# Block sums of the merge formed during the attention, another sequence of the seven products, output sums on VectorE

## The chip, the cores and the metric

One NeuronCore of one Trainium2 chip runs the whole kernel. The metric is the device time of one execution in microseconds (us). TensorE does the matrix products; VectorE (DVE in the rows), ScalarE (ACT) and GpSimd (POOL) work beside it, and SyncE (SP) issues nearly all transfers.

## What is computed

One layer of a hybrid mixer over 1024 tokens of width 1024, in float32. Four branches (A sparse, B sliding window, C stick-breaking, D retention) are gated, projected, merged and projected once more:

```python
h = rms_norm(x, norm_g) * (1.0 + scale) + shift
...
for i, (y, z) in enumerate(branches):
    yi = y.reshape(B, S, BRANCH_W) * jax.nn.silu(z)
    term = jax.nn.sigmoid(h @ w_merge[i]) * (yi @ w_br[i])
    merged = term if merged is None else merged + term
return x + gate * (merged @ w_out)      # and a last rms_norm with final_g
```

The four products `h @ w_merge[i]` and the last one with `w_out`, each 1024 x 1024 x 1024, are what the change is about.

## The kernel before

**Precision.** Every float32 factor is held as a sum of two parts, a rounded one (`hi`) and the rest (`lo`), and a product is three matmuls: hi·hi, hi·lo, lo·hi. To split a block of 128 x 512, ScalarE copies it into `hi` and VectorE or GpSimd subtracts to get `lo` (`parts`, line 1582; `op`, line 1623).

**Three stages.** First the attention stage: projections of `h` (called items), the attention units of the branches, and the z items, which multiply a branch by its gate and store A, B and D to DRAM (`yd`, line 666). Then the merge stage. Then the output stage with `w_out`.

**Seven products for eight.** In merge and output the 2 x 2 block product is done with seven block products instead of eight. The moving side (blocks b11, b12, b21, b22 of `h`, in `hh` and `hl`, line 1566) needs four sums of blocks: T1 = b12 - b11, T2 = b22 - T1, T3 = b22 - b12 and T4 = b21 - T2. `t_jobs` (line 1592) forms the first three when the merge stage begins, four slices of 512 columns each, in SBUF tiles `tt`; `t4_jobs` (line 1654) puts T4 in the place of b12 during the first pair. Because b12 is needed whole again at the end, its sum hi + lo is stored in DRAM (`hd`) and split again later (line 1841).

**The order of the merge.** The merge has 32 tiles of 128 output rows (4 branches x 8). Four of them (`PLAIN`, line 38) are done as ordinary products: two at the start (line 1720), two at the end (line 1826), 2 x (24 + 6) matmuls of 512 columns each. The other 28 are 14 pairs (line 1735); a pair is seven products of 12 matmuls (`product`, line 1679) and four terms of 6 (`br_term`, line 880). The sums of products of a pair are formed as they come out of PSUM: five additions on VectorE, two on GpSimd, and two copies on ScalarE.

**Output stage.** The four blocks of `w_out` are loaded into `wr` (line 1801) once the T tiles are free, that is after the fifth of the last pair's seven products (T3's). `w_jobs` (line 1800) forms their sums while the last two plain tiles run; some go where parts of `h` were, so they wait for the tile that read those. The output is then four pairs of seven products (line 1901). `gated` (line 1878) multiplies by the gate on VectorE and adds x, on GpSimd in three pairs of four; `norm` (line 1886) uses GpSimd for two multiplications and ScalarE for the scaling.

**What sets the order.** In each stage the program notes its instructions and `Program.schedule` (line 293) lists them by a cost model: at each step the engine that is free earliest takes its ready instruction of smallest rank. A rank is the place in the program plus a shift by label, from two long tables (`SHIFT_PE`, `SHIFT`, lines 99 to 151). What is issued is one fixed order for each engine, DMA issues on SP and GpSimd included. An instruction that waits holds up all that stands behind it on its engine.

Of the kernel before, what the change touches and what calls it, by code (L numbers as in the profile page):

```python
# [88 lines left out]
def chunks(w):  # L89
# [22 lines left out]
    ('first', 0): 300, ('first', 1): 0, ('first', 2): 300, ('first', 4): 9970, ('first', 5): 21923,  # L112
# [3 lines left out]
    ('h1', 7): 0, ('item', 0): 0, ('item', 10): 0, ('item', 11): 43, ('item', 12): 0,  # L116
    ('item', 13): 100, ('item', 14): -100, ('item', 16): -9900, ('item', 17): 10870,
    ('item', 19): 9990, ('item', 2): -10000, ('item', 21): 0, ('item', 22): 0, ('item', 26): 633,
    ('item', 28): 10000, ('item', 30): 9997, ('item', 4): -300, ('item', 5): 9997,
    ('item', 6): 9960, ('item', 7): 9967, ('item', 9): 2077, ('mod', 0): 0, ('mod', 1): 3000,  # L120
    ('mod', 2): 11000, ('mod', 3): 2900, ('mod', 4): -11000, ('mod', 5): -3, ('mod', 6): 0,
    ('mod', 7): 7000,
}
SHIFT = {
# [12 lines left out]
    ('D1', 5): 10173, ('D1', 6): 2990, ('ada', 3): -300, ('ada', 4): 10000, ('ada', 7): -30,  # L137
# [3 lines left out]
    ('item', 1): 10300, ('item', 10): -9910, ('item', 12): 20, ('item', 13): -10320,  # L141
    ('item', 14): -300, ('item', 15): -10997, ('item', 16): 9997, ('item', 18): 0,
    ('item', 19): 1100, ('item', 2): 0, ('item', 20): 0, ('item', 21): 0, ('item', 22): 273,
    ('item', 23): 0, ('item', 24): 100, ('item', 25): -10000, ('item', 26): 19676, ('item', 27): 0,
    ('item', 28): -9700, ('item', 29): -10000, ('item', 3): -3000, ('item', 30): 997,
    ('item', 4): 130, ('item', 5): 0, ('item', 6): 0, ('item', 7): 0, ('item', 8): -10643,
    ('item', 9): -10000, ('mod', 1): -11000, ('mod', 3): 0, ('mod', 4): 1000, ('mod', 5): -10800,
    ('mod', 6): -10980, ('mod', 7): -10000, ('split', 0): 0, ('split', 1): -10000,
    ('split', 2): -3000, ('split', 3): -10000, ('split', 4): -200, ('split', 6): 10300,
    ('split', 7): 21169, ('x', 4): 19990, ('x', 5): 10300, ('x', 6): 0, ('x', 7): -10000,  # L150
# [250 lines left out]
def hybrid_kernel(ctx: ExitStack, tc: tile.TileContext, x, c, w_ada, b_ada, norm_g, w_in, cmp_pos,  # L401
# [140 lines left out]
    hd = dram.tile([P, 4, 512], F32, name="hd")  # L542
# [288 lines left out]
    it_zcd = [z_item(c0 + P * p, br, p) for p in range(2) for br, c0 in (("C", C_Z), ("D", D_Z))]  # L831
# [43 lines left out]
    it_zb[1].after = "B1"  # L875

# [61 lines left out]
    with ac:  # L938
# [588 lines left out]
    with ExitStack() as mc:  # L1527
# [38 lines left out]
        hblk = [[[v[:, 4 * k:4 * k + 4, 512 * n:512 * n + 512] for v in (hh, hl)] for n in range(2)] for k in range(2)]  # L1566
        (b11, b12), (b21, b22) = hblk
# [4 lines left out]
        tstack = ctx.enter_context(ExitStack())  # L1572
        tt = tstack.enter_context(tc.tile_pool(name="tt", bufs=1, side="right")).tile([P, 3, 2, 4, 512], F32R, name="tt")
        T1, T2, T3 = [[tt[:, i, v] for v in range(2)] for i in range(3)]
# [11 lines left out]
        def minus(x, y, k, d, e):  # L1586

            ve.tensor_tensor(d, f(x[0][:, k]), f(y[0][:, k]), ALU.subtract)
            po.tensor_tensor(e, f(x[1][:, k]), f(y[1][:, k]), ALU.subtract)
            ve.tensor_tensor(d, d, e, ALU.add)  # L1590

        def t_jobs():

            for k in range(4):
                t1 = tmp(f"t1_{k}")
                minus(b12, b11, k, t1, tmp(f"t1e_{k}"))
                parts(T1, k, t1, ve)
                yield
                t2 = tmp(f"t2_{k}")
                ve.tensor_tensor(t2, f(b22[0][:, k]), t1, ALU.subtract)  # L1600
                ve.tensor_tensor(t2, t2, f(b22[1][:, k]), ALU.add)
                parts(T2, k, t2, ve)
                yield
            for k in range(4):
                t = tmp(f"b12_{k}")
                po.tensor_tensor(t, f(b12[0][:, k]), f(b12[1][:, k]), ALU.add)
                sy.dma_start(hd[:, k], t)
                t3 = tmp(f"t3_{k}")
                minus(b22, b12, k, t3, tmp(f"t3e_{k}"))
                parts(T3, k, t3, ve)  # L1610
                yield
# [11 lines left out]
        def op(n):  # L1623

            lo, hi = slice(0, 512), slice(512, 1024)
            if n < NP or n >= NP + 4:
                q, x = divmod(n if n < NP else n - NP - 4, 7)
                if n < NP:
                    (a11, a12), (a21, a22) = [[st.q[base + 2 * q + e].t[:, c] for c in (lo, hi)] for e in range(2)]
# [88 lines left out]
        with md.noted(tc, 8000.0):  # L1718
            tj = t_jobs()
            for n, _ in enumerate(run_items(it_m[:2])):  # L1720
                md.step += 1
                if n % 2 == 1:
                    next(tj, None)
# [276 lines left out]
```

## Time and profile before

| what | us |
|---|---|
| median of 3 runs (1114.05 to 1115.0) | 1114.21 |
| the profiled execution | 1112.57 |
| its span, first to last instruction | 1110.8 |

All rows below come from the one profiled execution, with times from its span's start. Its attention stage ends at about 584 us, the merge at about 1004 us. In the rows a name such as `mt<-hh` is output<-input tile, without buffer numbers: `hh`/`hl` hold the two parts of h, `tt` the T tiles, `mt` scratch, `wst` staged weights, `whi`/`wlo` their parts, `wr` the blocks of `w_out`, `w`/`wt` parts of its sums, `acc` the merged result, `z` rows of the output, `yd` the branches in DRAM. L346 and L369 are the lines that issue noted instructions; they are the same for all. A row of waits or idle time names what ended it.

### The profile page before, as it was taken

The page shows a single profiled execution, that of the slowest core. Times are in us where ns is not written, and L with a number is a line of the kernel's source. Part 1 is how long each engine was busy: PE and PEld are TensorE (multiplying, and loading weights), DVE is VectorE, ACT ScalarE, POOL GpSimd, SP SyncE. Part 2 cuts the span into 40 slices and gives each one's busy share as a digit, 9 for nine tenths or more (in the row PEclk, how much of TensorE's full clock was granted, in tenths as well). Part 3 has the DMA queues.
Part 4 walks back from the last instruction along what each step waited for, and adds up shares of the span by engine and source line. Part 5 has one row for each costly group of instructions (what it writes and reads, how often), then busy time and mean ns, then how long its engine had stood idle before and what let it go on. Part 6 is the DMA issues. An engine that isn't in the chain of part 4 may idle for free.

```text
span 1110.8 us, 16056 instructions
## 1 busy us (share of the span) xinstructions
PE 1043.6 (94%) x5391; PEld 877.6 (79%) x5391; DVE 840.1 (76%) x1753; ACT 589.7 (53%) x1293; POOL 600.2 (54%) x591
## 2 busy tenths in 40 slices
PE   5799999999999999999999699999999999995985
PEld 3578887889888888888888478888888888884874
DVE  6868995987467777878849986677785565668998
ACT  4378974995357667768753343333343333344443
POOL 4584214303444556536555653466666566667785
PEclk9799999999999999999999899999999999997998
DMA  9834311103331010113031023322232233331231
GB/s 299 243 114 119 67 39 39 35 8 75 52 86 48 10 49 30 31 33 81 20 98 60 34 62 105 107 69 67 86 91 54 51 90 86 103 134 59 93 115 76
DMA packets 120230, 86.59 MB, mean 78 GB/s; under 512 B 14556, under 2 KB 107796, under 8 KB 120148
## 3 DMA queue, kind: packets, MB, share of 16 engines
q1 hardware_dynamic: 118672, 81.07, 25.7%
q0 software_dynamic: 1408, 4.48, 1.3%
q8 instruction: 42, 0.69, 0.3%
q14 instruction: 40, 0.33, 0.1%
q10 hardware_dynamic: 68, 0.02, 0.0%
HBM read 72.45 MB, written 8.39 MB: 73 GB/s over the span
## 4 chain that ended last, share of the span: by engine, by line
PE 57%; DVE 10%; issue 3%; ACT 2%; POOL 1%; POOLq 0%; ACTq 0%; DVEq 0%
PE d L346 21%; PE s L346 18%; PE t L346 12%; PE y L346 7%; DVE mt L346 4%; DVE acc L346 1%; DVE wlo L346 1%; DVE hl L346 1%; DVE hl L369 1%; DVE tt L346 0%; DVE SP L346 0%; POOL wlo L346 0%; DVE z L346 0%; POOL mt L346 0%; ACT whi L346 0%
## 5 line engine op out<-in xcount | busy, mean ns | idle before, releaser
L346 POOL TENSOR_TENSOR wlo<-wst,whi 128x512 fp32r<-128x512 f32 (+1 forms) x108 | 141.1, 1317 | 154.6 <-ACT whi L346 140.2
L346 PE MATMUL d<-hh,whi 128*128 128x512 f32 x440 | 182.4, 414 | 16.2 <-ACT whi L346 12.6
L346 PE MATMUL d<-hh,wlo 128*128 128x512 f32 x440 | 174.5, 397 | 1.2 <-POOL wlo L346 1.2
L346 PE MATMUL d<-hl,whi 128*128 128x512 f32 x440 | 173.9, 396 | 0.2 <-POOL hl L346 0.2
L346 ACT ACTIVATE whi<-wst 128x512 fp32r<-128x512 f32 (+2 forms) x121 | 89.0, 737 | 117.7 <-DMA wst<-in_w_merge_dram 35.2
L346 PEld LDWEIGHTS d<-hh,whi 128*128 128x128 f32 x440 | 84.0, 191 | 29.6 <-ACT whi L346 13.5
L346 PEld LDWEIGHTS d<-hh,wlo 128*128 128x128 f32 x440 | 83.4, 190 | 20.9 <-POOL wlo L346 1.6
L346 POOL TENSOR_SCALAR SP<-SP,den,gates 128x640 f32<-128x640 f32 (+7 forms) x64 | 49.8, 787 | 86.7 <-DVE den L346 49.5
L346 PEld LDWEIGHTS d<-hl,whi 128*128 128x128 f32 x440 | 84.2, 191 | 12.0 <-POOL hl L346 0.7
L346 DVE TENSOR_TENSOR lo<-t,hi 128x512 fp32r<-128x512 f32 (+2 forms) x132 | 80.5, 624 | 15.7 <-ACT hi L346 14.8
L346 ACT ACTIVATE hi<-t 128x512 fp32r<-128x512 f32 (+3 forms) x148 | 75.2, 526 | 32.2 <-PE t L346 23.5
L346 PE MATMUL s<-hh,whi 128*128 128x512 f32 x200 | 79.3, 396 | 1.0 <-ACT whi L346 1.0
L346 PE MATMUL s<-hh,wlo 128*128 128x512 f32 x200 | 78.5, 393 | 1.8 <-DVE wlo L346 1.8
L346 POOL TENSOR_TENSOR acc<-acc,mt 128x512 f32<-128x512 f32 x44 | 68.1, 1547 | 19.8 <-DVE mt L346 18.9
L346 PE MATMUL s<-hl,whi 128*128 128x512 f32 x200 | 78.1, 392 | 0.0
L346 ACT ACTIVATE SP<-SP,mx 128x257 f32<-128x257 f32 (+9 forms) x96 | 62.3, 651 | 28.7 <-DVE mx L346 22.9
L346 PE MATMUL t<-kbt,SP 128*128 128x128 f32 (+1 forms) x470 | 69.4, 273 | 8.6 <-DMA kbt<-in_kb_dram 6.9
L346 ACT ACTIVATE mt<-mt 128x512 f32<-128x512 f32 x56 | 35.1, 628 | 65.8 <-POOL mt L346 48.4
L346 PEld LDWEIGHTS t<-kbt,SP 128*128 128x128 f32 (+1 forms) x470 | 55.5, 141 | 16.0 <-DMA kbt<-in_kb_dram 6.9
L346 PE MATMUL s<-tt,whi 128*128 128x512 f32 x176 | 55.7, 398 | 2.9 <-ACT whi L346 2.9
L346 POOL TENSOR_TENSOR mt<-mt,mt 128x512 f32<-128x512 f32 x34 | 49.9, 1467 | 9.0 <-DVE mt L346 7.8
L346 ACT ACTIVATE t<-t 128x512 f32<-128x512 f32 (+5 forms) x97 | 50.2, 524 | 1.3
(365 smaller groups left out, 2946.2 us busy)
## 6 DMA issues: line engine op xcount, KB each, us to landing
wst<-in_w_merge_dram SPq DMA_DIRECT2D x32, 512.0 KB, 4.3
wst<-in_w_in_dram SPq DMA_DIRECT2D x26, 512.0 KB, 3.8
FA<-in_w_ada_dram SPq DMA_DIRECT2D x10, 512.0 KB, 6.0
FA<-in_x_dram SPq DMA_DIRECT2D x8, 512.0 KB, 4.7
pst<-in_w_br_dram SPq DMA_DIRECT2D x32, 128.0 KB, 2.2
ga<-in_w_ada_dram SPq DMA_DIRECT2D x16, 256.0 KB, 3.0
wr<-in_w_out_dram SPq DMA_DIRECT2D x4, 1024.0 KB, 9.1
z<-in_x_dram SPq DMA_DIRECT2D x8, 512.0 KB, 3.8
```

The source lines that it names most:

```text
L346: fn(*args, **kw)
L369: return f(*a, **k)
```

## The change

1. **Block sums in the attention stage.** `t_unit` forms all four sums, slice by slice, after the second z item, splits them and stores both parts in DRAM (`td`, 32 stores of 256 KB). Its scratch is the room of branch D's results, so the z items of D now come ahead of those of C. b12's two parts are stored as they are (`hd`, 2 stores of 1 MB). At the start of the merge six loads of 1 MB bring T2, T1 and T3 into SBUF; two bring T4 over b12 after the two plain tiles; two bring b12 back near the end, without a new split. `t_jobs` and `t4_jobs` are gone.
2. **Another sequence of the products.** T3's product comes third and T1's fifth (`TURN`). All seven sums are VectorE additions with an input in PSUM; the two GpSimd additions and one of the ScalarE copies are gone.
3. **w_out.** T1 has a room of its own; the room of T2 and T3 is given up after the last pair's third product, and the four loads of `w_out` are noted there, ahead of its other four products. w11's parts go over T1. The sum of blocks that was formed twice per slice in scratch is formed in place.
4. **Output.** `gated` is VectorE alone; `norm` is one VectorE instruction over 1024 columns in place of two on GpSimd and one on ScalarE.
5. **Order.** Both tables of shifts are new, and there are labels for the merge and output instructions (`op`, `out`, `tile`, `w`, `sums`).

```diff
 SHIFT_PE = {
...
-    it_zcd = [z_item(c0 + P * p, br, p) for p in range(2) for br, c0 in (("C", C_Z), ("D", D_Z))]
+    it_zcd = [z_item(c0 + P * p, br, p) for br, c0 in (("D", D_Z), ("C", C_Z)) for p in range(2)]
...
+    def t_unit(k):
+        lo, hi = slice(0, 512), slice(512, 1024)
+        d, e, th, tl = Fs[1][:, lo], Fs[1][:, hi], Fs[3][:, lo], Fs[3][:, hi]
+        def f(x, v):
+            return x[v][:, k].bitcast(F32)
+        def put(i, t):
+            se.activation(th.bitcast(F32R), t, AF.Copy)
+            ve.tensor_tensor(tl.bitcast(F32R), t, th, ALU.subtract)
+            for v, s in enumerate((th, tl)):
+                sy.dma_start(td[i, v, :, k], s)
+        ve.tensor_tensor(d, f(b22, 0), f(b12, 0), ALU.subtract)
+        po.tensor_tensor(e, f(b22, 1), f(b12, 1), ALU.subtract)
+        ve.tensor_tensor(d, d, e, ALU.add)
+        put(2, d)
+        for v in range(2):
+            ve.tensor_tensor(d, d, f(b11, v), ALU.add)
+        put(1, d)
+        for i, x in ((0, b22), (3, b21)):
+            ve.tensor_tensor(e, f(x, 0), d, ALU.subtract)
+            ve.tensor_tensor(e, e, f(x, 1), ALU.add)
+            put(i, e)
...
+            if it is it_zcd[1]:
+                for v in range(2):
+                    sy.dma_start(hd[v], b12[v].bitcast(F32))
+                for k in range(4):
+                    md.label = "sums", k
+                    t_unit(k)
...
+        TURN = (0, 1, 4, 3, 2, 5, 6)
...
+            add(u2, o, t1)
+            o = product(7 * q + 2, MOVING[4])
...
+            add(u3, o, u2)
+            yield
+            o = product(7 * q + 3, MOVING[3])
...
+            add(g11, o, t1)
...
+            o = product(7 * q + 4, MOVING[2])
+            op(7 * q + 7)
+            add(t1, o, u2)
+            add(c5, o, u3)
...
+            for i, t in ((1, T2), (0, T1), (2, T3)):
+                for v in range(2):
+                    sy.dma_start(f(t[v]), td[i, v])
...
+            for v in range(2):
+                sy.dma_start(f(b12[v]), td[3, v])
+            for q in range(len(pairs)):
+                rest = pair(q)
+                next(rest)
+                if q + 1 < len(pairs):
+                    for _ in rest:
+                        pass
...
+            for t, kh, n in ((r11, 0, 0), (r12, 0, 1), (r22, 1, 1), (r21, 1, 0)):
+                sy.dma_start(t, wo_v[:, 4 * kh:4 * kh + 4, 512 * n:512 * n + 512])
+            for _ in rest:
+                pass
...
-                        for k in range(4):
-                            t = tmp(f"b12r_{k}")
-                            sy.dma_start(t, hd[:, k])
-                            parts(b12, k, t, ve)
+                        for v in range(2):
+                            sy.dma_start(f(b12[v]), hd[v])
...
-        def gated(z, cs, t, e=po, d=ve):
-            d.tensor_tensor(t, t, gateb[:, cs], ALU.mult)
-            add(z[:, cs], z[:, cs], t, e)
+        def gated(z, cs, t):
+            ve.tensor_tensor(t, t, gateb[:, cs], ALU.mult)
+            add(z[:, cs], z[:, cs], t)
...
-            for cs in (lo, hi):
-                po.tensor_tensor(z[:, cs], z[:, cs], fgb[:, cs], ALU.mult)
-            se.activation(z, z, AF.Copy, scale=s[:, 5:6])
+            ve.scalar_tensor_tensor(z, z, s[:, 5:6], fgb, op0=ALU.mult, op1=ALU.mult)
```

## Rows read from the trace of the kernel before

**Rows 1.** The page, part 1: busy us (share of the span) x instructions.
```profile
PE 1043.6 (94%) x5391; PEld 877.6 (79%) x5391; DVE 840.1 (76%) x1753; ACT 589.7 (53%) x1293; POOL 600.2 (54%) x591
```

**Rows 2.** Windows: length, busy us (x count) by engine, granted clock, DMA share, GB/s.
```profile
600.00:620.00 20.00, 16.06 (x65) 12.51 (x64) 19.99 (x20) 4.82 (x10) 14.96 (x10) 0.93 0.16 60
620.00:640.00 20.00, 13.26 (x43) 9.47 (x43) 18.76 (x22) 6.50 (x12) 10.45 (x7) 0.81 0.05 14
640.00:660.00 20.00, 17.85 (x71) 13.95 (x70) 18.73 (x25) 7.23 (x12) 10.71 (x8) 0.91 0.15 46
...
1000.00:1020.00 20.00, 8.39 (x34) 5.90 (x33) 20.00 (x22) 7.99 (x15) 15.78 (x8) 0.75 0.01 2
...
1040.00:1060.00 20.00, 19.78 (x87) 15.94 (x85) 19.96 (x22) 9.46 (x18) 17.28 (x13) 1.00 0.31 106
```

**Rows 3.** Windows of the attention's second half and of the pairs, same columns.
```profile
300.00:580.00 280.00, 278.08 (x1671) 243.41 (x1670) 208.86 (x730) 188.11 (x499) 144.12 (x208) 1.00 0.16 46
...
640.00:980.00 340.00, 337.85 (x1490) 279.08 (x1489) 225.29 (x316) 124.86 (x225) 204.13 (x155) 0.99 0.30 87
```

**Rows 4.** The chain that ended last, in order of time: start us, us, what.
```profile
684.34 5.44 PE s L346 x24
...
1004.58 5.07 DVE hl L369 x3
...
1013.58 1.08 DVE s L346
...
1018.85 5.34 PE d L346 x12
```

**Rows 5.** Timeline of PE: first merge matmul, first, twelfth and thirteenth output matmul, last.
```profile
584.64 0.39 PE L346 MATMUL s<-hh,whi 128*128 128x512 f32 x1
...
1004.14 0.63 PE L346 MATMUL t<-w,whi 128*128 128x512 f32 x2
...
1006.84 0.40 PE L346 MATMUL t<-w,wlo 128*128 128x512 f32 x1
1018.85 0.80 PE L346 MATMUL d<-hh,whi 128*128 128x512 f32 x1 [11.61 <-ACT whi L346]
...
1098.87 0.28 PE L346 MATMUL s<-wt,wlo 128*128 128x256 f32 x1
```

**Rows 6.** Groups by form, DVE, 588 to 660 us: xcount | busy us, mean ns.
```profile
L346 DVE TENSOR_TENSOR mt<-hh 128x512 f32<-128x512 f32 x8 | 15.5, 1947 | 1.4 <-POOL FA L346 1.4
L346 DVE TENSOR_TENSOR tt<-mt,tt 128x512 fp32r<-128x512 f32 x12 | 13.3, 1118 | 1.4 <-ACT tt L346 1.2
L346 DVE TENSOR_TENSOR mt<-mt,mt 128x512 f32<-128x512 f32 x12 | 8.1, 678 | 0.0
```

**Rows 7.** Groups by form, DVE, 300 to 580 us.
```profile
L346 DVE TENSOR_TENSOR lo<-t,hi 128x512 fp32r<-128x512 f32 x70 | 47.2, 686 | 9.0 <-ACT hi L346 8.2
```

**Rows 8.** Last store of a branch (timeline of POOL); transfers into tile wr, x4.
```profile
588.70 0.58 POOL L346 DMA_DIRECT2D yd<-FA  x1 [0.30 <-POOL FA L346]
...
DMA to landing us min/median/max: 5.1/9.1/13.0
```

**Rows 9.** Groups by form, DVE, 1019 to 1099 us.
```profile
L346 DVE TENSOR_TENSOR wlo<-acc,whi 128x512 fp32r<-128x512 f32 x22 | 23.5, 1070 | 3.7 <-ACT whi L346 3.6
L346 DVE TENSOR_TENSOR mt<-mt,wst 128x512 f32<-128x512 f32 x15 | 20.1, 1345 | 0.0
...
L346 DVE TENSOR_TENSOR mt<-s,mt 128x512 f32<-128x512 f32 x8 | 5.5, 682 | 0.3 <-PE s L346 0.3
```

**Rows 10.** Groups by form, POOL, 1019 to 1099 us.
```profile
L346 POOL TENSOR_TENSOR z<-z,mt 128x512 f32<-128x512 f32 x13 | 21.2, 1629 | 5.1 <-DVE mt L346 5.0
```

**Rows 11.** Timeline of DVE: start us, us, what [idle before].
```profile
982.65 0.69 DVE L346 SCALAR_TENSOR_TENSOR mt<-mt,y 128x512 f32<-128x512 f32 x1 [6.18 <-PE y L346]
...
1016.85 0.68 DVE L346 TENSOR_TENSOR wlo<-s,whi 128x512 fp32r<-128x512 f32 x1
1017.46 0.68 DVE L346 TENSOR_TENSOR acc<-s,acc 128x512 f32<-128x512 f32 x1
...
1104.54 0.75 DVE L346 SCALAR_TENSOR_TENSOR z<-z,ssq,wst 128x512 f32<-128x512 f32 x1
```

More of the change, by code (lines that the diff above doesn't have):

```diff
@@ L147 @@
[L147 to L150, printed above, removed]
[13 rows of a table added]
+    ('ada', 6): 20000, ('ada', 7): 0, ('first', 7): 0, ('h0', 0): 70, ('h0', 1): -9980,
+    ('h0', 2): 12783, ('h0', 3): -7000, ('h0', 5): -1000, ('h0', 7): 0, ('h1', 0): -10000,
@@ L151 @@
+    ('out', 94): 10, ('out', 95): 0, ('out', 96): 300, ('split', 0): -10300, ('split', 1): -960,
+    ('split', 3): -9897, ('split', 4): 20000, ('split', 5): -10000, ('split', 6): -10100,
+    ('split', 7): 9200, ('sums', 0): 9633, ('sums', 1): 10390, ('sums', 2): 10307,
+    ('sums', 3): 18717, ('tile', 15): -10, ('tile', 23): -9900, ('tile', 31): 10,
[5 rows of a table added]
 }
@@ L875, in hybrid_kernel @@
     it_zb[1].after = "B1"
+    hblk = [[[v[:, 4 * k:4 * k + 4, 512 * n:512 * n + 512] for v in (hh, hl)] for n in range(2)] for k in range(2)]
+    (b11, b12), (b21, b22) = hblk
+    def t_unit(k):
[19 more added lines that the diff above has]
+            put(i, e)
     it_m = []
@@ L1571, in hybrid_kernel @@
         fstack.close()
-        tstack = ctx.enter_context(ExitStack())
-        tt = tstack.enter_context(tc.tile_pool(name="tt", bufs=1, side="right")).tile([P, 3, 2, 4, 512], F32R, name="tt")
-        T1, T2, T3 = [[tt[:, i, v] for v in range(2)] for i in range(3)]
+        tstack = ExitStack()
+        tps = [s.enter_context(tc.tile_pool(name=n, bufs=1, side="right")) for s, n in ((ctx, "tp1"), (ctx.enter_context(tstack), "tp23"))]
+        tt = [tps[i > 0].tile([P, 2, 4, 512], F32R, name=f"tt{i}") for i in range(3)]
+        T1, T2, T3 = [[t[:, v] for v in range(2)] for t in tt]
         def tmp(name):
@@ L1649, in op @@
                 st.dma_upto(base + 2 * q + 4)
+            md.label = label
         keep = [tmp(f"keep{i}") for i in range(6)]
         t1, u2, c5, g11 = keep[:4]
-        def t4_jobs():
-            for k in range(4):
-                d, e = ((g11, keep[4]), (keep[5], g11))[k % 2]
-                minus(b21, T2, k, d, e)
-                parts(b12, k, d, ve)
-                yield
         def y_load(q, n):
@@ L1680, in product @@
             oh, ol = ops[n % 4]
+            md.label = "out", n
             o = pools["g"].tile([P, 512], F32, name=f"w{n}_{cs.start}", tag="g")[:, 0:cs.stop - cs.start]
@@ L1716, in gate_end, with pair @@
                     sy.dma_start(gd.rearrange("(k p) -> p k", p=P), gatec)
+        def pair(q):
+            i, j = pairs[q]
+            u3 = keep[4 + q % 2]
+            first, fin = j == 0, q + 1 < len(pairs) and pairs[q + 1][1] == 0
+            o = product(7 * q + 0, MOVING[0])
+            if q:
+                term(q - 1, 1, 0, keep[4 + (q - 1) % 2])
+                pwprep(8 * i + 2 * j + 1)
+                if first:
+                    y_part(q, 0)
+                    y_load(q, 1)
+            op(7 * q + 3)
+            se.activation(t1, o, AF.Copy)
+            gate_load(q - 1, 0)
+            o = product(7 * q + 1, MOVING[1])
+            op(7 * q + 4)
+            add(u2, o, t1)
+            o = product(7 * q + 2, MOVING[4])
+            if first:
+                y_part(q, 1)
+            op(7 * q + 5)
+            add(u3, o, u2)
+            yield
+            o = product(7 * q + 3, MOVING[3])
+            op(7 * q + 6)
+            add(g11, o, t1)
+            tanh(g11)
+            gate_sum(q - 1, 0)
+            gate_load(q - 1, 1)
+            o = product(7 * q + 4, MOVING[2])
+            op(7 * q + 7)
+            add(t1, o, u2)
+            add(c5, o, u3)
+            term(q, 0, 0, g11)
+            o = product(7 * q + 5, MOVING[5])
+            op(7 * q + 8)
+            add(t1, o, t1)
+            tanh(c5)
+            term(q, 1, 1, c5)
+            gate_sum(q - 1, 1)
+            if fin:
+                y_load(q + 1, 0)
+            o = product(7 * q + 6, MOVING[6])
+            op(7 * q + 9)
+            add(u3, o, u3)
+            tanh(t1)
+            term(q, 0, 1, t1)
+            tanh(u3)
+            gate_end(q - 1)
+            i2, j2 = pairs[q + 1] if q + 1 < len(pairs) else (3, 3)
+            pwprep(8 * i2 + 2 * j2)
         with md.noted(tc, 8000.0):
-            tj = t_jobs()
+            for i, t in ((1, T2), (0, T1), (2, T3)):
+                for v in range(2):
+                    sy.dma_start(f(t[v]), td[i, v])
             for n, _ in enumerate(run_items(it_m[:2])):
                 md.step += 1
-                if n % 2 == 1:
-                    next(tj, None)
                 if n == 24:
@@ L1791, in hybrid_kernel @@
+            for v in range(2):
[6 more added lines that the diff above has]
+                        pass
         tstack.close()
         rstack = ctx.enter_context(ExitStack())
-        r = rstack.enter_context(tc.tile_pool(name="wr", bufs=1, side="right")).tile([P, 4, 4, 512], F32, name="wr")
-        r11, r12, r21, r22 = [r[:, i] for i in range(4)]
@@ L1795, in hybrid_kernel @@
-        w11 = mc.enter_context(tc.tile_pool(name="w11", bufs=1)).tile([P, 2, 4, 512], F32R, name="w11")
-        w11 = [w11[:, v] for v in range(2)]
+        wr = rstack.enter_context(tc.tile_pool(name="wr", bufs=1, side="right"))
+        (r11, r12), (r21, r22) = [[t[:, n] for n in range(2)] for t in [wr.tile([P, 2, 4, 512], F32, name=f"wr{k}") for k in range(2)]]
+        w11 = T1
         wo_v = w_out[0].rearrange("(k p) c -> p k c", p=P)
@@ L1800, in w_jobs @@
         def w_jobs():
-            for t, kh, n in ((r11, 0, 0), (r12, 0, 1), (r22, 1, 1), (r21, 1, 0)):
-                sy.dma_start(t, wo_v[:, 4 * kh:4 * kh + 4, 512 * n:512 * n + 512])
-            for _ in range(4):
-                yield
             for k in range(4):
@@ L1811, in w_jobs @@
                 yield
+            for k in range(4):
+                ve.tensor_tensor(r11[:, k], r12[:, k], r11[:, k], ALU.add)
+                yield
             for _ in range(4):
@@ L1850, in hybrid_kernel @@
                         op(NP + 5 + 2 * e)
+            md.label = "w", 32
             for _ in wj:
```

172 lines of the change are left out of this document (56 added, 116 removed), and 65 rows, old and new, of tables (SHIFT, SHIFT_PE).

## The prediction

> **What bounds the kernel now.** I read the page first: TensorE is busy for 94% of the span [rows 1], so a change that leaves its matmuls alone, as this one does, can only win back idle or slow TensorE time. Next, the windows of 20 us: they show where that time is. Between 600 and 660 TensorE issues 65, 43 and 71 matmuls per window while VectorE is busy for 20.0, 18.8 and 18.7 us; between 1000 and 1020 it issues 34 while VectorE is busy for all 20.0 [rows 2]. The granted clock falls to 0.93, 0.81, 0.91 and 0.75 there: after TensorE pauses, part of its work runs at the lower level, 1.2 GHz. In the second half of the attention and in the pairs TensorE is busy for 278.1 of 280 and 337.9 of 340 us [rows 3]. So the limit is TensorE, except at two places, where it is VectorE.
>
> What these places cost comes from the pace. In the chain of waits 24 matmuls take 5.44 us, 0.227 us each [rows 4]. From the first merge matmul at 584.6 to the first output matmul at 1004.1 there are 419.5 us [rows 5]; the work is 120 + 14 x 108 + 120 = 1752 matmuls, 397.1 us, so 22.4 are lost. Of these, 600 to 660 loses 60 - 179 x 0.227 = 19.4 (the records of that stretch are all of the wide kind). The output's 28 products, 336 wide matmuls' worth, need 76.2 us and take 95.0, from 1004.1 to 1099.1: 18.8 lost. Of that 11.6 is one wait ahead of the thirteenth matmul [rows 5]; the twelve matmuls after it take 5.34 us for 2.72 [rows 4], 2.6 lost to the clock, and the twelve ahead of it 3.1, another 0.4; 4.2 are spread over the four output pairs. After the last matmul come 11.7 us of tail.
>
> **First place: the block sums leave the merge.** T1 to T4 are 12 VectorE instructions for each of four slices, 48 in all. Three groups alone hold 32 of them, 36.9 us busy [rows 6]; the other 16, at the 0.68 us of the shortest, make 10.9 more: 48 of the stretch's 72 us. They go, with 12 of GpSimd's 16. In their place stand six loads of 1 MB. Four such loads landed 5.1 to 13.0 us after issue [rows 8], so six need about 19.5 us. Their room holds the last branch results until the store at 588.7 [rows 8] is done, a few us later; all have landed by about 611. The two plain tiles need no T and at full pace last until 584.6 + 27.2 = 611.8; T2 is wanted 2.7 us later, T3 another 2.7, T1, now fifth, later still. So the loads are hidden by the plain tiles. If that cover is gone, because SP holds them behind a wait, 10 us of stall come back: the first four, issued at 611.8, land at 624.8 against 614.5. What stands behind them on SP is the pair's own weights. T4's two loads wait for the plain tiles to end and have six products, 16 us, against about 7. I take 2 us of the 19.4 as staying (ends 0 and 10): **-17.4**.
>
> **Price of that in the attention.** The 48 instructions now run there, with 16 ScalarE copies, 4 GpSimd subtractions and 34 stores on SP. VectorE is busy for 208.9 of the 280 us, so 71.1 are free; ScalarE has 92 free; the DMA share is 0.16, and 10 MB more over some 200 us is half as much again [rows 3]. Priced at the 0.686 us of the same shape there [rows 7] the sums take 33 us, at the 1.118 that splits took in the merge [rows 6] 54. Both fit into 71, but not all idle time is usable: VectorE's order is fixed, and a sum that waits for its copy holds up a softmax behind it, on which TensorE's transposes wait. TensorE idles for 1.9 of the 280 us now. I let that grow to about 2% of the stretch, **+4** (ends 0 and 18: the latter if only half of the idle time is usable and each costs 1.118, 54 - 36).
>
> **The pairs.** Two more VectorE additions each, two GpSimd ones and a copy fewer. An addition with an input in PSUM takes 0.68 us beside busy GpSimd too [rows 9]; 28 of them are 19 us in a stretch where VectorE has 115 of 340 free and TensorE has no gaps [rows 3]. Cost 0: TensorE's own work hides it; without that cover 1.4 us per pair.
>
> **Second place: w_out.** The wait ends on VectorE: at 1004.6 it is in splits of w_out's blocks, and the sum for the second output product, whose inputs are older, only comes at 1013.6 because it stands behind them in the queue [rows 4]. The change moves the loads two products and their terms earlier, so the four differences and four sums can run where VectorE sits idle now, such as the 6.2 us ahead of 982.7 [rows 11]; the four splits of b12 are gone. That is 12 instructions out of the way, at 20.0 us for 22 in that window [rows 2] 10.9 us of the 11.6. w11 needs T1's room, free after the fifth product: still ahead of the plain tiles. The two loads of b12 (2 MB) are issued after the last product and have two plain tiles, 13.6 us, beside what is left of w_out's four. Of 11.6 + 2.6 + 0.4 I let 3 stay (ends 0 and 11.6, if the order still puts the splits first): **-11.6**.
>
> **Output pairs.** VectorE is busy for 19.96 of 20 us there already [rows 2], and the change gives it more: per pair two PSUM additions, four additions on z and two norms of 1024 columns. Its instructions today fall into two kinds. With an input in PSUM: 0.68. With both inputs in SBUF: 1.07 and 1.35 [rows 9], but 0.68, with 0.61 between starts, at 1016.9 [rows 11], where GpSimd is idle. The long ones lie beside GpSimd's 1.63 us additions [rows 10], which go. Without them a pair is 11 splits and sums of the operands, 7 additions, 8 for gate and x, 26 x 0.61, and two norms, each twice the 512-column one (0.75 [rows 11]), 2 x 1.22: 18.3 us, against 84 x 0.227 = 19.0 on TensorE. It fits, barely, and I keep the 4.2 us of losses: **0** (ends -4 and +4). The Trainium skill (Perfetto Trace Analysis, Optimizing Scalar/DVE Operations) speaks against this part: where VectorE is saturated, work should go off it. It adds that GpSimd shares a port with it, so that moving work between those two might not help. By the first half the output would grow, which is the slower rival below; the two kinds of rows side with the second.
>
> **Tail and order tables.** The tail gets two instructions more on VectorE and two fewer on GpSimd: 0 (ends -2 and +1.5). The new shifts in the attention's first half cannot be priced from rows; all TensorE idle time is 67 us, about half of it accounted for above: 0 (ends -5 and +5).
>
> **Sum:** -17.4 + 4 + 0 - 11.6 = -25.0. Against the profiled execution's 1112.6 that is 1087.6; that execution stands 1.6 below the median of 1114.2, so for the median **1089**.
>
> **The rivals.**
> - *The attention pays more.* VectorE at 86 to 94% busy holds up the units: +18 in place of +4, 1103. For it: VectorE is the busiest engine there after TensorE. Against: 71 us free.
> - *One stall stays.* The T loads late (+8) or the splits of w_out still ahead of the first sums (+8.6): 1097 to 1098. For it: both hang on one fixed order.
> - *All of it goes right.* Both stalls, the 4.2 us and the attention's price vanish: 1089 - 2 - 3 - 4 - 4 = 1076. For it: nothing else in the merge holds up TensorE.
> - *Slower: VectorE bounds the output.* Place: the four output pairs. If instructions with two SBUF inputs stay long without GpSimd, at the mean 1.18 of the two groups [rows 9], 1.11 between starts, a pair is 7 x 0.61 + 19 x 1.11 + 2.4 = 27.8 us: 8.8 over TensorE, 35 in four pairs, 1124. It beats the gain from 25.5 us per pair on, a spacing of 0.99 for those 19. For it: VectorE is full there now, and the same sum for today's 5 and 15 instructions gives 19.7, near today's pace. Against: the 0.68 beside idle GpSimd.
> - *Nothing gained.* The sums run last in the attention, the loads wait for them, and the first stall only changes its name while the second stays: about 1114.
>
> **How the numbers follow.** Forecast (1080 to 1097) 0.45; attention or one stall 0.25; all right 0.2; slower 0.06; nothing gained 0.04. The unknown ends, among them 5 us either way for the tables, carry the second and third cases to 1106 and 1075: range 1075 to 1106, leaving out about 2 in 10. This kernel's measurement tells 0.2%, 2.2 us, from no change: faster 0.9, same 0.03, slower 0.07.
>
> **What would show it.** Right: 86 to 88 wide matmuls per 20 us in the first 60 us after the plain tiles, at clock 1.00; no wait over 3 us at the first output products; instructions with two SBUF inputs near 0.68 us in the output; the first merge matmul at 584 to 590. Wrong: that matmul after 600 (the attention paid), a wait of TensorE on `tt` with a DMA as its end, VectorE full with TensorE waiting in each output pair, or the 11.6 us wait still there under another name.

## The result: 1099.05 us, and the profile after

The changed kernel takes **1099.05 us** (median of 4 runs, 1097.74 to 1100.75) against 1114.13 of the kernel before in the same comparison; the ratio is 0.987, 95% interval 0.9852 to 0.9888. The forecast was 1089, with a range of 1075 to 1106: the side and the range hold, but the gain is 15 us where 25 were expected. All times below are from single profiled executions; that of after took 1097.74, with a span of 1096.0.

The page of after, part 1; to be read against [rows 1]:

```profile
PE 1041.4 (95%) x5391; PEld 874.2 (80%) x5391; DVE 821.6 (75%) x1803; ACT 575.7 (53%) x1265; POOL 490.8 (45%) x519
```

The same matmuls; GpSimd lost 109 us of work, VectorE has 50 instructions more and yet 18.5 us less busy time. Where TensorE won and lost is in the windows of after, columns as in [rows 2, 3]:

```profile
300.00:580.00 280.00, 274.19 (x1632) 236.51 (x1632) 232.53 (x778) 193.30 (x512) 152.94 (x210) 1.00 0.25 74
...
600.00:620.00 20.00, 20.00 (x90) 16.57 (x89) 5.79 (x11) 2.24 (x4) 3.38 (x4) 1.00 0.97 364
620.00:640.00 20.00, 16.69 (x67) 12.95 (x66) 9.97 (x13) 6.22 (x11) 6.24 (x5) 0.91 0.56 182
640.00:660.00 20.00, 20.00 (x90) 16.57 (x89) 9.75 (x16) 6.88 (x12) 4.73 (x5) 1.00 0.12 33
...
1000.00:1020.00 20.00, 12.94 (x44) 9.22 (x43) 13.82 (x18) 8.58 (x16) 7.91 (x6) 0.83 0.42 157
...
1040.00:1060.00 20.00, 20.00 (x90) 16.58 (x89) 19.71 (x33) 8.07 (x17) 0.55 (x1) 1.00 0.34 126
```

The attention is worse (TensorE busy for 274 of 280 us, 278 before); the merge's start has one dent left, the output's start another; the output's pairs run at full pace, 90 matmuls in 20 us. The timeline of TensorE in after gives the borders of the stages, as [rows 5] did (first merge matmul, the merge's one long wait, first output matmul, the output's one long wait, the 34th output matmul, from which TensorE runs at full pace, last matmul):

```profile
593.36 0.39 PE L372 MATMUL s<-hh,whi 128*128 128x512 f32 x1
...
624.71 1.22 PE L372 MATMUL d<-tt,whi 128*128 128x512 f32 x2 [3.31 <-ACT whi L372]
...
999.70 0.61 PE L372 MATMUL t<-tt,whi 128*128 128x512 f32 x2
...
1012.25 0.79 PE L372 MATMUL s<-hh,whi 128*128 128x512 f32 x1 [6.34 <-ACT whi L372]
...
1017.52 0.39 PE L372 MATMUL d<-hh,whi 128*128 128x512 f32 x1
...
1086.23 0.28 PE L372 MATMUL s<-wt,wlo 128*128 128x256 f32 x1
```

From such rows of each run comes this table (us; the attention ends with the first merge matmul, the output runs from its first matmul to the end of its last, the tail from there to the span's end). The rows below the second are the experiments that follow, but for two whose attention was planned anew (they stand under their headings).

| kernel | attention | merge | output | tail | time |
|---|---|---|---|---|---|
| before | 584.6 | 419.5 | 95.0 | 11.7 | 1112.6 |
| after | 593.4 | 406.3 | 86.8 | 9.5 | 1097.7 |
| sums one column wide | 591.6 | 406.6 | 87.2 | 9.5 | 1096.6 |
| sums formed in the merge | 593.6 | 418.8 | 86.1 | 9.5 | 1109.8 |
| T1 behind the weights | 593.4 | 400.9 | 86.3 | 9.5 | 1091.8 |
| fifth block's split later | 594.7 | 407.4 | 84.5 | 9.4 | 1097.9 |
| fifth product in its place | 591.9 | 407.4 | 87.8 | 11.2 | 1100.1 |
| before, output on VectorE | 586.6 | 417.8 | 91.7 | 10.8 | 1108.6 |
| w_out loads noted late | 596.0 | 409.0 | 85.5 | 9.4 | 1101.7 |
| T1 behind, w_out on VectorE | 593.6 | 400.4 | 83.1 | 9.4 | 1088.3 |
| the same, fifth in its place | 593.0 | 400.4 | 81.2 | 11.2 | 1087.5 |

What ended last, in the chain of waits of after (start us, us, what; the first two in the attention, the next three around the merge's dent, the rest at the output):

```profile
295.98 4.87 DMA SP<-in_cmp_w_dram
...
324.37 4.11 DMA RA<-RA
...
603.89 17.80 DMA wst<-in_w_merge_dram
...
621.71 0.70 DVE s L372
...
624.71 4.75 PE d L372 x12
...
1008.19 1.22 DVE yl L395 x2
...
1009.49 0.56 ACT wt L372
...
1010.54 1.14 ACT wt L372 x2
1011.68 0.53 ACT whi L372
...
1012.25 5.43 PE s L372 x12
```

Three readings follow, each tested below. The attention waits for transfers at 296 and 324, long before the sums. The merge waits for pair 0's second weight tile, which landed 17.8 us after its issue, behind six T loads. The output waits for an operand that ScalarE splits late, behind the split of w_out's fifth block (`wt`), which itself waits for VectorE's last reads of w_out's blocks (`yl`).

### The profile page after: what moved, and what is told of

Same layout as the page of the kernel before. It is cut to its first block, busy times and chain, and to the rows that moved or that the text cites. A ratio compares the mean times of both kernels' runs of the same rounds, so it can differ in the third digit from the quotient of the medians.

```text
span 1096.0 us, 16030 instructions
## 1 busy us (share of the span) xinstructions
PE 1041.4 (95%) x5391; PEld 874.2 (80%) x5391; DVE 821.6 (75%) x1803; ACT 575.7 (53%) x1265; POOL 490.8 (45%) x519
## 4 chain that ended last, share of the span: by engine, by line
PE 77%; DVE 10%; ACT 4%; DMA 4%; issue 2%; POOL 1%; SPq 1%; POOLq 0%; DVEq 0%; ACTq 0%
PE d L372 30%; PE s L372 22%; PE t L372 15%; PE y L372 9%; DVE SP L372 3%; DMA wst<-in_w_merge_dram 2%; ACT t L372 1%; DVE lo L372 1%; DVE FA L372 1%; ACT SP L372 1%; SPq L372 1%; DVE yl L395 1%; DMA SP<-in_w_ada_dram 1%; DVE acc L372 1%; DMA FA<-in_x_dram 1%
## 5 line engine op out<-in xcount | busy, mean ns | idle before, releaser
L372 POOL TENSOR_TENSOR wlo<-wst,whi 128x512 fp32r<-128x512 f32 (+1 forms) x108 | 145.2, 1354 | 175.3 <-ACT whi L372 173.4
L372 PEld LDWEIGHTS d<-hl,whi 128*128 128x128 f32 x440 | 83.1, 189 | 10.6
L372 DVE TENSOR_TENSOR lo<-t,hi 128x512 fp32r<-128x512 f32 (+2 forms) x132 | 80.6, 623 | 11.9 <-ACT hi L372 10.9
L372 POOL TENSOR_SCALAR SP<-SP,den,gates 128x640 f32<-128x640 f32 (+7 forms) x64 | 53.0, 837 | 75.1 <-DVE den L372 25.5
L372 DVE TENSOR_TENSOR mt<-s,mt 128x512 f32<-128x512 f32 x61 | 41.2, 686 | 33.9 <-PE s L372 33.7
L372 PE MATMUL s<-tt,whi 128*128 128x512 f32 x192 | 59.1, 389 | 0.0
```

The lines of the kernel that those rows point to most:

```text
L372: fn(*args, **kw)
```

## The experiments

### What the attention pays for

**The sums' arithmetic left out.** The 32 stores stay; each copies a part of h.

```diff
-        ve.tensor_tensor(d, f(b22, 0), f(b12, 0), ALU.subtract)
...
+        for i, x in ((2, b22), (1, b11), (0, b22), (3, b21)):
+            for v in range(2):
+                sy.dma_start(td[i, v, :, k], f(x, v))
```

> The code after, without the arithmetic of the block sums: the 32 stores to the spare DRAM block stay, but each copies a part of h there as it is, so that T1 to T4 hold blocks of h and the output is another one. The first matmul of the merge (s<-hh,whi) began at 584.6 us in the kernel before and at 593.4 us in the kernel after. Theory A, VectorE's 48 added operations hold up the attention: without them it begins by 587 us. Theory B, the new order tables (another order of the interleaved work of the attention) cost the 8.7 us: it begins at 591 us or later all the same.

Measured, in a single execution: 1121.93 us, 23 us longer than after with less work. The timeline of TensorE in this run, its first merge matmul:

```profile
615.04 0.39 PE L372 MATMUL s<-hh,whi 128*128 128x512 f32 x1
```

This can't be read as the price of the arithmetic in either direction. The list scheduler plans the attention from the noted instructions and the tables; with 68 instructions gone it gave another order for all of it.

**The tables of before.**

```diff
-    ('A0', 0): -100, ('A0', 1): 10, ('A0', 10): 10030, ('A0', 11): 0, ('A0', 12): 100,
...
+    ('A0', 0): -10000, ('A0', 1): 1967, ('A0', 11): -300, ('A0', 12): -10000, ('A0', 13): 0,
...
```

> The code after, with the order tables of the kernel before for every label that both have; those that only the new code has (the last pair's weights, the sums) keep theirs. Nothing is computed otherwise. Theory B, the order tables cost the attention 8.7 us: the merge's first matmul is back at 585 to 588 us and the time falls by 5 to 8 us, to about 1092 us. Theory A, the added VectorE work costs them: it stays near 593 us, and the time within 2 us of 1099.

Measured: 1181.9 us, ratio to before 1.0615 (1.0585 to 1.0644); the first merge matmul stands at 669.2. Neither theory had that. So the old tables don't carry over to the new list of instructions: new code with them is 83 us slower than with its own. The two runs show that a price of the order can't be found by editing what is planned; the plan has to be held still.

**The plan held still, the sums one column wide when issued.**

```diff
+        def thin():
+            for i in range(at, len(md.ops)):
+                for n, (fn, a, kw) in enumerate(md.ops[i].calls):
+                    if fn.__name__ != "dma_start":
+                        md.ops[i].calls[n] = fn, [x[:, 0:1] if isinstance(x, bass.AP) else x for x in a], kw
```

> The code after with its plan unchanged, instruction for instruction on every engine; only, once the plan is made, the block sums' arithmetic (12 operations in each of four units on VectorE, ScalarE's copies, GpSimd's differences) is issued one column wide in place of 512, so the sums are not computed and the output is another one; the 32 stores stay whole. Removing the arithmetic ahead of the plan gave another plan and a first merge matmul at 615.0 us, which told nothing of the arithmetic's cost; this one does. Theory A, VectorE's added work costs the attention its 8.7 us: the first merge matmul, 593.4 us in the kernel after, begins by 587 us. Theory B, the new order of the attention's work costs them: it begins at 591 us or later.

Measured, in a single execution: the first merge matmul at 591.60. Seven runs with the full sums and this same attention (after and six of the runs below) have it at 591.9 to 596.0, mean 593.7; the two with the attention of before at 584.6 and 586.6, mean 585.6. So of some 8 us about 2 are the sums, no more than the spread between executions, and 6 what the plan changed: theory B. Windows show the same: first before, then after, then this run.

```profile
300.00:380.00 80.00, 79.36 (x454) 67.86 (x452) 57.43 (x203) 49.49 (x131) 36.70 (x51) 1.00 0.19 50
380.00:580.00 200.00, 198.72 (x1219) 175.55 (x1218) 151.44 (x528) 138.62 (x369) 107.42 (x157) 1.00 0.15 44
```
```profile
300.00:380.00 80.00, 75.40 (x432) 62.94 (x432) 56.33 (x208) 49.38 (x135) 36.19 (x55) 1.00 0.25 60
380.00:580.00 200.00, 198.79 (x1202) 173.57 (x1202) 176.20 (x571) 143.92 (x378) 116.75 (x155) 1.00 0.25 80
```
```profile
300.00:380.00 80.00, 75.56 (x433) 62.95 (x432) 56.40 (x209) 49.41 (x135) 36.29 (x55) 1.00 0.26 60
380.00:580.00 200.00, 199.44 (x1216) 175.48 (x1214) 155.39 (x572) 138.55 (x380) 104.73 (x157) 1.00 0.26 83
```

TensorE loses 4 us of busy time between 300 and 380, with sums or without, and the first sum starts only at 379.4. (Counted by the columns of its matmuls, at 0.227 us for 512, after's TensorE is 0.3 us of work behind before's at 300 us, 7.2 at 380.) From 380 to 580 VectorE is busy for 176 of 200 us in after, 155 with thin sums, and TensorE gets 1202 and 1216 matmuls done. The plan differs from before's by its tables and by D's z items ahead of C's; which of these makes the transfers at 296 and 324 late is open. It wasn't tried, as every edit of the plan moves all of it.

### The start of the merge

**T1 behind the second weight tile.**

```diff
-            for i, t in ((1, T2), (0, T1), (2, T3)):
+            for i, t in ((1, T2), (2, T3)):
...
+                    for v in range(2):
+                        ve.tensor_copy(T1[v][:, 0, 0:1], st.q[base + 1].t[:, 0:1])
+                        sy.dma_start(f(T1[v]), td[0, v])
                     op(0)
```

> The code after, with T1's two loads issued behind pair 0's second weight tile instead of ahead of it (a one-column copy out of that weight tile into T1 makes them wait for it); T2 and T3 are loaded first. Theory: the 3.3 us wait of the merge at 624.7 us, and the 2.0 us that the twelve matmuls behind it lost, come of 6 MB of block sums standing ahead of that weight tile: both go, and the time falls by about 5 us, to about 1094. Rival: that tile would be late in any case, or T1 is now late itself by as much: no change within 2 us.

Measured: 1091.83 us, ratio 0.9795 (0.9781 to 0.981), 7.2 us below after (5.4 us less in the merge of the profiled execution). Its windows and, below, SP's timeline:

```profile
600.00:620.00 20.00, 20.00 (x90) 16.58 (x89) 7.64 (x16) 2.82 (x6) 3.39 (x4) 1.00 0.84 290
620.00:640.00 20.00, 20.00 (x90) 16.58 (x89) 10.70 (x17) 7.10 (x13) 6.63 (x6) 1.00 0.74 255
```
```profile
600.10 1.99 SPq L372 DMA_DIRECT2D tt<-td  x4
...
603.14 0.45 SPq L372 DMA_DIRECT2D wst<-in_w_merge_dram  x1
...
617.57 0.94 SPq L372 DMA_DIRECT2D tt<-td  x2
```

The dent is gone and the merge takes 400.9 us. T1's 2 MB, issued at 617.6, are still in time for the fifth product. So the late tile was the cause, and the six loads ahead of it made it late: the DMA share of after was 0.97 in 600 to 620, so what stood last in that row came last.

**The sums back in the merge.**

```diff
-            for i, t in ((1, T2), (0, T1), (2, T3)):
-                for v in range(2):
-                    sy.dma_start(f(t[v]), td[i, v])
+            tj = t_jobs()
...
+                if n % 2 == 1:
+                    next(tj, None)
```

> The code after, with T1, T2 and T3 formed at the start of the merge and T4 in its first pair, as in the kernel before, and no copies of them in DRAM; the sequence of products stays the new one. Its attention is planned anew without the sums, which moves its end by an amount unknown ahead (it was 615.0 us where the sums' arithmetic was left out of the plan), so only the merge is read: from its first matmul to the output's first it takes 406.3 us in the kernel after and 419.5 in the kernel before (584.6 to 1004.1). Theory: the sums cost the merge their stall again, 415 to 420 us. Rival: the new sequence of products hides them, and the move itself gained little: 405 to 409 us.

T4's scratch in this run lies over a sum that the new sequence of products still holds, so part of the output differs. Measured, in a single execution: the merge takes 418.8 us (its attention, planned without sums, ends at 593.6, with the same tables that gave 615.0 above), and its windows are those of [rows 2] again:

```profile
620.00:640.00 20.00, 12.26 (x41) 8.53 (x40) 19.97 (x23) 5.48 (x10) 10.87 (x7) 0.90 0.07 20
640.00:660.00 20.00, 18.02 (x69) 13.22 (x68) 17.89 (x26) 8.28 (x14) 8.09 (x6) 0.93 0.18 52
```

The theory holds: moving the sums is worth 12.5 us in the merge, and the new sequence of products, with its additions on VectorE, alone (418.8 against 419.5) nothing there.

### The output

**The fifth block's split later on ScalarE.**

```diff
-            md.label = "wt4", 0
-            for k in range(4):
-                parts(wt4, k, t4f[k], po)
...
+                if q == 0:
+                    md.label = "wt4", 0
+                    oh = ops[(b + 4) % 4][0]
+                    se.activation(wt4[0][:, :, 0:1], f(oh[:, 0:4]).rearrange("p (k c) -> p k c", c=1), AF.Copy)
+                    for k in range(4):
+                        parts(wt4, k, t4f[k], po)
```

> The code after, with the splitting of the last pair's fifth weight block (four copies on ScalarE and their differences on GpSimd) noted one product later, behind the first output pair's later operand, and made to wait for that operand by a one-column copy on ScalarE. Theory: the 6.3 us wait of the output at 1012.3 us, and the 2.7 us that the twelve matmuls behind it lost, come of ScalarE standing at those four copies, which wait for VectorE to finish with the block: most of it goes, and the time falls by 6 to 9 us, to about 1091. Rival: something else is as late (VectorE's own operands of the second product): a fall of under 2 us.

The loads of the gate now overwrite that block before it is split, so that weight holds other values. Measured: 1095.66 us, ratio 0.984 (0.9816 to 0.9865), 3 us below after where 6 to 9 were expected. The four executions lie at 1093.5, 1093.8, 1097.6 and 1097.9 and the interval overlaps that of after, so these 3 us are not clear of the noise. In the profiled one the output takes 84.5, 2.3 less than in after; its attention and merge are 2.5 longer. The wait became two, the second on VectorE (timeline of TensorE):

```profile
1010.38 0.50 PE L372 MATMUL s<-hh,whi 128*128 128x512 f32 x1 [2.02 <-ACT whi L372]
...
1013.08 0.79 PE L372 MATMUL s<-hh,wlo 128*128 128x512 f32 x1 [1.93 <-DVE wlo L372]
```

**The fifth product back in its place.**

```diff
-    ('mod', 4): 370, ('mod', 7): 300, ('out', 102): -10000, ('out', 103): 330, ('out', 106): -10030,
+    ('mod', 4): 370, ('mod', 7): 300, ('out', 102): -10000, ('out', 103): 330,
```

> The code after, with one entry of its order tables taken out, that of the fifth product of the first output pair, which the tables had drawn forward to stand third on TensorE; it then stands fifth. (With ScalarE's copies of the fifth weight block moved behind that product's operand instead, the wait only fell from 6.3 to 2.0 plus 1.9 us, VectorE's part of the operand being as late.) Theory: the operand of that product (the sum s of two blocks, VectorE's work) can't be there 6 us into the output, whatever ScalarE does, and the two products put behind it have theirs: the 6.3 us wait at 1012.3 us and the 2.7 us of slow matmuls behind it go, the time falls by 7 to 9 us, to about 1091. Rival: the products drawn forward in its place wait as long for their own operands: a fall of under 3 us.

Measured: 1100.16 us, ratio 0.9872 (0.9855 to 0.989): nothing gained, the theory fell. In its place stand waits of TensorE for VectorE's `wlo` (us in total, times, longest; one of the three on `s`, 0.9 us, is in the merge, as in after):

```profile
PE s L372 <- DVE wlo L372: 3.0, 3, 1.7
PE d L372 <- DVE wlo L372: 2.7, 1, 2.7
```

The granted clock is 0.76 from 1020 to 1030, and the tail 11.2. So with another order the waits end on VectorE's part of the operands. The one entry moved more than that product: several later ones stand elsewhere, and the last product's matmuls are split around another's, so this run doesn't price the one product alone.

**Before, with the output's sums on VectorE.**

```diff
-            d.tensor_tensor(t, t, gateb[:, cs], ALU.mult)
-            add(z[:, cs], z[:, cs], t, e)
+            ve.tensor_tensor(t, t, gateb[:, cs], ALU.mult)
+            add(z[:, cs], z[:, cs], t)
...
+            ve.scalar_tensor_tensor(z, z, s[:, 5:6], fgb, op0=ALU.mult, op1=ALU.mult)
...
-                e = ve if q == 3 else po
+                e = ve
...
```

> The kernel before with only the third part of the change: gate products, sums and the final scaling of the output on VectorE. The output before lost 4.2 us in its eight products' pairs beyond the stall at its start and had a tail of 11.7 us; after has none of the first and a tail of 9.5. Theory: VectorE without GpSimd beside it does the added work at 0.68 us an operation and has room: 4 to 6 us less than before, about 1108 to 1110. Rival (mine of the prediction): the operations stay near 1.2 us, VectorE bounds the output and the time is above 1118. Nothing else is left out.

Measured: 1108.54 us, ratio 0.9949 (0.9933 to 0.9965), a gain of 5.9 on before in the same comparison. The groups of VectorE by form in the output, this run from 1022 us and then after from 1018, columns as in [rows 9]:

```profile
L346 DVE TENSOR_TENSOR wlo<-acc,whi 128x512 fp32r<-128x512 f32 x21 | 15.3, 742 | 3.9 <-ACT whi L346 3.9
L346 DVE TENSOR_TENSOR mt<-mt,wst 128x512 f32<-128x512 f32 x15 | 11.2, 754 | 0.1
L346 DVE TENSOR_TENSOR z<-z,mt 128x512 f32<-128x512 f32 x15 | 10.2, 688 | 0.1
```
```profile
L372 DVE TENSOR_TENSOR wlo<-acc,whi 128x512 fp32r<-128x512 f32 x20 | 13.4, 684 | 0.0
L372 DVE TENSOR_TENSOR mt<-mt,wst 128x512 f32<-128x512 f32 x16 | 11.5, 724 | 0.2
L372 DVE TENSOR_TENSOR z<-z,mt 128x512 f32<-128x512 f32 x15 | 10.1, 685 | 0.0
L372 DVE SCALAR_TENSOR_TENSOR z<-z,ssq,wst 128x1024 f32<-128x1024 f32 x6 | 7.7, 1279 | 0.1
```

Operations with two SBUF inputs fell from 1070 and 1345 ns [rows 9] to 742 and 754 in this run and to 684 and 724 in after, with GpSimd out of the way. The slower rival is false.

**w_out's loads noted late.**

```diff
-            for t, kh, n in ((r11, 0, 0), (r12, 0, 1), (r22, 1, 1), (r21, 1, 0)):
-                sy.dma_start(t, wo_v[:, 4 * kh:4 * kh + 4, 512 * n:512 * n + 512])
             for _ in rest:
                 pass
+            for t, kh, n in ((r11, 0, 0), (r12, 0, 1), (r22, 1, 1), (r21, 1, 0)):
+                sy.dma_start(t, wo_v[:, 4 * kh:4 * kh + 4, 512 * n:512 * n + 512])
```

> The code after, with w_out's four loads noted behind the last four products of the last pair instead of ahead of them. Read is the output from its first product to its last matmul's end: 95.0 us in the kernel before, 86.8 after, 91.7 where before has only the output's sums on VectorE. Theory: the loads (4 MB, some 11.7 us at the 345 GB/s that they move) have to be on their way one product group early to be split in time; noted later, w11's parts come late and the merge waits by the last tiles or the output starts with a longer stall: the merge and the output together take 5 to 10 us more than the 493.1 us of the kernel after. Rival: the planner issues them as soon as their buffer is free wherever they are noted, and that the last pair's products end early is what counts: within 2 us of 493.1.

Measured in a single execution: merge and output take 494.5 us against 493.1: the rival holds. The first load is issued at 957.28 instead of 954.56, but this run's merge also begins 2.6 us later: from the first merge matmul it is 361.3 us here and 361.2 in after. So the place where the loads are noted hardly moved them. That it is the early release of their room that lets them go then is what the rival says; no run kept the room longer.

**w_out's differences on VectorE, on top of T1 behind the weights.**

```diff
-                parts(w11, k, r11[:, k], po)
+                parts(w11, k, r11[:, k], ve)
...
-                po.tensor_tensor(r12[:, k], r22[:, k], r12[:, k], ALU.subtract)
+                ve.tensor_tensor(r12[:, k], r22[:, k], r12[:, k], ALU.subtract)
...
-                po.tensor_tensor(t4f[k], r21[:, k], r11[:, k], ALU.subtract)
+                ve.tensor_tensor(t4f[k], r21[:, k], r11[:, k], ALU.subtract)
...
-            parts(b12, k, r21[:, k], po)
+            parts(b12, k, r21[:, k], ve)
```

> The code of the run with T1 behind pair 0's second weight tile (1091.8 us), and on top of it w_out's sixteen differences of the last pair on VectorE instead of GpSimd (four halves of its first block, two times four differences of blocks, four halves of the fourth). Taking the drawn-forward product back moved the output's wait from ScalarE's operand to VectorE's and gained nothing, so the theory now is: VectorE is behind, being 19.7 of 20 us busy in 980 to 1000 us, where eight of its operations take 1.66 to 1.78 us in place of 0.68 while GpSimd runs; its sixteen operations cost VectorE 16 x 0.6 = 9.6 us and give back about 10 us of those longer ones and GpSimd's own 1.3 to 1.7 us each. The wait of 6.3 us at the output shrinks by 2 to 5 us and the time falls to 1087 to 1090. Rival: VectorE's queue only gets longer, and the wait stays or grows: 1091 to 1095.

Measured: **1088.13 us**, ratio 0.9761 (0.9745 to 0.9777), 3.7 below the run it stands on and better than both kernels. The window of after, that of this run, and TensorE's wait in this run:

```profile
980.00:1000.00 20.00, 20.00 (x90) 16.57 (x89) 19.73 (x21) 10.59 (x17) 15.68 (x10) 1.00 0.00 1
```
```profile
980.00:1000.00 20.00, 18.93 (x84) 15.35 (x82) 19.96 (x34) 10.98 (x20) 0.00 (x0) 1.00 0.00 1
```
```profile
1002.73 0.80 PE L372 MATMUL s<-hh,whi 128*128 128x512 f32 x1 [3.79 <-ACT whi L372]
```

VectorE is full in both, but does 34 instructions instead of 21 (GpSimd did 10 beside them). In after the same operation takes 1.78 us beside one of GpSimd and 0.68 without (timelines of GpSimd and VectorE):

```profile
982.93 1.83 POOL L372 TENSOR_TENSOR acc<-acc,mt 128x512 f32<-128x512 f32 x1
983.53 1.78 DVE L372 TENSOR_TENSOR acc<-acc,mt 128x512 f32<-128x512 f32 x1
...
991.59 0.68 DVE L372 TENSOR_TENSOR acc<-acc,mt 128x512 f32<-128x512 f32 x1
```

Six of the 21 take 1.66 to 1.78 us (the expectation's eight are those from 978 to 1003). From 960 to 1010 the mean of this operation is, in after and then in this run:

```profile
L372 DVE TENSOR_TENSOR acc<-acc,mt 128x512 f32<-128x512 f32 x4 | 4.9, 1231 | 0.0
```
```profile
L372 DVE TENSOR_TENSOR acc<-acc,mt 128x512 f32<-128x512 f32 x4 | 2.7, 681 | 0.0
```

The wait is 3.8 us instead of 6.3, as expected; VectorE is still late, only less.

**The same with the fifth product in its place.**

```diff
-    ('mod', 4): 370, ('mod', 7): 300, ('out', 102): -10000, ('out', 103): 330, ('out', 106): -10030,
+    ('mod', 4): 370, ('mod', 7): 300, ('out', 102): -10000, ('out', 103): 330,
```

> The same, and the first output pair's fifth product back in its place. Theory (VectorE's backlog, not the order alone): with the backlog smaller the natural order pays, as every operand now comes in the order in which it is formed: 1 to 4 us below the run without it, about 1086. Rival (the planner's drawn-forward order is right for the real durations too): the same or slower than that run.

Measured: 1088.33 us, ratio 0.9766 (0.9752 to 0.9781): the same as without. The output is 1.9 us shorter (81.2) and the tail 1.8 longer (11.2). The tail is 11.2 in both runs without that entry and 9.4 to 9.5 in after and all the other runs of the table that keep its output; in both, the last product's matmuls are split around another's, so the longer tail goes with the order at the end. Whether the start alone, in the natural order, would have won the 1.9 us is open.

## Why the prediction was right, and where its sum was not

The bound was read rightly: TensorE, and VectorE at two places. But the terms, measured by the table of stages, are these:

| step, as the prediction put it | expected | measured |
|---|---|---|
| price in the attention, with order tables | +4, 0 | +8.7 |
| first place, block sums leave the merge | -17.4 | -13.2 |
| second place, w_out | -11.6 | -4.1 |
| output pairs | 0 | -4.1 |
| tail | 0 | -2.1 |
| sum | -25.0 | -14.8 |

The 8.2 us that the output won are split by its trace. Before, the first 24 matmuls took 19.9 us in place of 5.4 (1004.14 to 1024.03), 14.4 lost; after, the first 33 took 17.8 in place of 7.5 (999.70 to 1017.52), 10.3 lost. What is spread over the rest fell from 4.4 to 0.3.

That the time lies well inside the range is in part luck. Attention, merge and w_out together missed their terms by 16.4 us, and 6.2 came back from the pairs and the tail, for which the sum had nothing.

**The attention: the term for the order tables, 0 with ends of -5 and +5, failed**, and by more than its end. The sums cost about 2 us, less than the 4 put on them; VectorE's idle time took them in. The new plan costs about 6, between 300 and 380 us, where the chain has two transfers of 4.9 and 4.1 us. The prediction gave the tables no price because no row had one; the two runs with other plans of nearly the same work end the attention 22 and 76 us later.

**The first place: "What stands behind them on SP is the pair's own weights" is the step that failed.** It was named and priced at nothing. The loads themselves were hidden by the plain tiles, as said: no matmul waited for `tt`. The 17.8 us of the weight tile behind them cost a wait of 3.3 us, and twelve matmuls that took 4.75 us for 2.72; putting T1 behind it brought the merge's gain from 13.2 to 18.6, above the 17.4 forecast. That the rest of the gain comes of the move itself, and none of it of the new sequence, the run with the sums in the merge shows.

**The second place: the mechanism was right, the size was not.** VectorE was to be freed by 12 instructions out of the way; the step that failed is their worth, "10.9 us of the 11.6". The four differences and four sums did come early (966 to 982 us), yet VectorE is full again from 980 to 1000: sixteen differences run on GpSimd between 961 and 1002, beside which VectorE's operations with two SBUF inputs take up to 1.78 us instead of 0.68. The prediction used just that to clear the output pairs, and didn't apply it to the stretch ahead of them. The rival "one stall stays" named this as the splits of w_out still ahead of the first sums; that is what is seen, at 6.3 + 2.7 us.

**The output pairs and the tail** were kept at no gain out of caution. Their own reckoning (18.3 us of VectorE for 19.0 of TensorE) was right, and implied the 4 us at its favourable end; the run with this part alone gives 3.3 in the output and 0.9 in the tail. The Trainium skill (Perfetto Trace Analysis, Optimizing Scalar/DVE Operations) says that taking work off a full VectorE may make sense, and that moving it between VectorE and GpSimd might not help, as they share a port. Here it helped twice, towards VectorE: the kernel before became 5.9 us faster with its output's work there, the kernel with T1 behind the weights 3.7 us with w_out's differences there. The Trainium skill (SBUF — State Buffer, SBUF: two separate sides) says that a VectorE operation with two SBUF inputs waits for a GpSimd operation that reads SBUF and began first to end, rather than share with it; the rows of 1.78 and 0.68 us fit that.

Of the signs listed, the 0.68 us and the wait on `tt` that did not come were right. The matmuls per window came to 67 at clock 0.91 in the first 20 us after the plain tiles and to 90 only from 640 on; the first merge matmul at 593.4 missed 584 to 590, and the wait of over 3 us at the output is there, under the same name.

## What to carry to other kernels

When transfers are moved to a stage's start, count what is queued behind them and by when it is wanted, not only whether they are hidden themselves: sorting two of six loads behind one weight tile was worth 7 us. Where VectorE is late, look first at what GpSimd does beside it: taking 16 GpSimd operations into VectorE's full queue made VectorE faster. And where a planner with fitted tables orders the work, cost an edit only with the plan held still; any other run measures the plan.

## What was not expected of the hardware

That a full VectorE does more by taking more on: 34 instructions in 20 us without GpSimd, 21 beside it, or 31 with GpSimd's ten. That a tile of 512 KB, issued 0.6 us behind 6 MB at up to 364 GB/s, lands 17.8 us later, after all that stands ahead of it. And that VectorE at 88% busy (176 of 200 us, 380 to 580) held TensorE up by no more than some 2 us beyond what it did at 78%.
